# Where two pools begin in SBUF: activations 96 bytes, the MLP's stationary tiles 32 bytes past a multiple of 512

## The chip, the cores and the metric

The kernel runs on one core of one Trainium2 chip. The metric is the device time of one execution in microseconds (us); the median of two runs before the change is 1291.11 us (1289.03 and 1293.18).

## The reference

One decoder layer on x of 256 tokens by 2048, all in float32:

```
h   = x @ w_in                       # 2048 -> 7424
y_a = rwkv7_mix(h[:, :3328])         # 16 heads of 64: decay, in-context rate, state update, norm, gate
y_b = retention_mix(h[:, 3328:])     # 4 heads of 256: rotary, decayed scores, norm, swish gate
mix = concat(y_a, y_b) @ w_o         # 2048 -> 2048
x   = layer_norm(ALPHA * x + mix)
ff  = square(relu(x @ w_up)) @ w_down  # 2048 -> 8192 -> 2048
out = layer_norm(ALPHA * x + ff)
```

## The kernel before, in words

All weight matrices are streamed once from HBM as 202 chunks of 128 x 2048 floats (1 MB). A chunk comes as two halves: SP's queue loads a half into one of three `raw` tiles, ScalarE casts it to float32r as `whi` (L133), and VectorE writes the rest `raw - whi` as `wlo` (L135). `prefetch` (L119 ff.) keeps about one chunk ahead. Activations are held in the same two parts (`xh`/`xl` for x, `mxh`/`mxl` for the mixer's output, `x1h`/`x1l` after the first norm, `u0` and `uh`/`ul` for the squared ReLU), so a product of two matrices takes three TensorE matmuls for each 128 x 128 block: high by high, high by low, low by high. Every one of them comes with its own load of a stationary operand of 128 columns, 512 bytes in each partition.

Two forms carry nearly all of TensorE's time, and they differ in which side is stationary:

- `stat_tile` (L151): the weight block is stationary, and 256 columns of an activation move past it (1024 bytes per partition). 48 matmuls a chunk. Used for most of the input projection (40 tiles, `xh`/`xl`, 1920 matmuls; two more tiles at L377) and for the MLP's up projection (60 tiles, `x1h`/`x1l`, 2880 matmuls).
- `mov_chunk` (L167): 128 columns of an activation are stationary, and 512 columns of the weights move (2048 bytes). 24 matmuls a chunk. Used for retention's v and g (`xh`/`xl`, 384), for the output projection (`mxh`/`mxl`, 288), and for the MLP's down projection (`u0`, 96; `uh`/`ul`, 1344). `resident_block` (L187) is the same form for three blocks whose weights stay in SBUF as `wx` or `wb`.

In order of time: the input projection with the two mixers woven in (to about 453 us; their vector work runs on the other engines), the output projection (to about 556), the first norm and the first 512 columns of the up projection (to 586), then the MLP in four slices: L151 on `x1h`/`x1l`, then L167 on `uh`/`ul`, four times (586 to 1259); the last 512 output columns at L187 and the second norm end it.

Where a tile begins is set by the pools: each is laid out behind the pool before it, and each tile begins at a multiple of 32 bytes. Before the change the pool `big` holds four buffers of 16 KB under one tag; they are taken in turn by `xh`, `xl`, `mxh`, `mxl`, then `x1h`, `x1l`, `u0` and, at the end, the four `wb`. The pools behind it (`rp` of the mixers; `mp`, `wx`, `mp2` of what follows) begin where `big` ends; `mp` holds `stats2`, of which 60 of 108 floats are used.

Of the kernel before, what the change touches and what calls it, by code (L numbers as in the profile page):

```python
# [10 lines left out]
F32 = mybir.dt.float32  # L11
F32R = mybir.dt.float32r
# [5 lines left out]
P = 128  # L18
T = 256
D = 2048  # L20
KT = D // P
# [52 lines left out]
WO_ORDER = ((0, (0, 2)), (1, (0, 2)), (0, (1, 3)), (1, (1, 3)), (2, (0, 1, 2, 3)))  # L74
NS = 4

WO_LAST = 58 + 12

LAG = dict(lora=2, scan=3, sq=5, rn=1, kk=7, bt=2, g1=1, btok=1, ktok=2, g2=1, sub=3, xt=2, vtok=8, bg=4, d1=3, d2=1, f1=1, sa=2, st=2, yc=2)
# [21 lines left out]
def tile_hybrid_layer(ctx, tc, xT, xtok, ws, pp, lup, glup, ln1r, ln2r, cst, rope, dmask, eye, out):  # L101
# [2 lines left out]

    const = ctx.enter_context(tc.tile_pool(name="const", bufs=1))
    wp = ctx.enter_context(tc.tile_pool(name="wp", bufs=1))
    big = ctx.enter_context(tc.tile_pool(name="big", bufs=4))
    ps = ctx.enter_context(tc.tile_pool(name="ps", bufs=4, space=bass.MemoryType.PSUM))

    def mm_bank():  # L110
        return ps.tile([P, 512], F32, name="mm", tag="mm", bufs=4)

    def sm_bank():
        return ps.tile([P, 512], F32, name="sm", tag="sm", bufs=4)
# [6 lines left out]
    def prefetch(want=1):  # L121
        while len(ahead) < want and taken[0] < ws.shape[0]:
# [7 lines left out]
            for h, (hi, lo) in enumerate(parts):  # L130
                raw = wp.tile([P, 1024], F32, name="raw", tag="raw", bufs=3)
                nc.sync.dma_start(out=raw, in_=ws[i][:, 1024 * h:1024 * h + 1024])
                S.copy(hi, raw)  # L133
                E = G if (i - WO_LAST, h) in LO_G else V
                E.tensor_tensor(out=lo, in0=raw, in1=hi.bitcast(F32), op=ALU.subtract)  # L135
# [22 lines left out]
    def mov_chunk(act, dsts, first, last):  # L158

        ch = chunk()  # L160
        for tt in range(2):
            for k4 in range(4):
                hi, lo = ch[k4 // 2]
                c = slice(512 * (k4 % 2), 512 * (k4 % 2) + 512)
                ah, al = act(k4, tt)
                for j, (w, a) in enumerate(((hi, ah), (hi, al), (lo, ah))):
                    TE.matmul(dsts[tt], a, w[:, c], start=first and k4 == 0 and j == 0,  # L167
                              stop=last and k4 == 3 and j == 2)
                if tt == 1 and k4 == 1:
                    prefetch()  # L170
                if k4 % 2:
                    yield
# [22 lines left out]
    ppt = const.tile([P, NPP], F32, name="ppt")  # L195
    nc.scalar.dma_start(out=ppt, in_=pp)
    c1 = const.tile([P, NC1], F32, name="c1")
    xh = big.tile([P, KT * T], F32R, name="xh", tag="big")
    xl = big.tile([P, KT * T], F32R, name="xl", tag="big")
    def xact(kt):  # L200
        return xh[:, kt * T:kt * T + T], xl[:, kt * T:kt * T + T]

    def tok_act(ah, al, kq):
        def f(k4, tt):
            o = (4 * kq + k4) * T + P * tt
            return ah[:, o:o + P], al[:, o:o + P]
        return f

    mxh = big.tile([P, KT * T], F32R, name="mxh", tag="big")
    mxl = big.tile([P, KT * T], F32R, name="mxl", tag="big")  # L210

    ident = c1[:, C_ID:C_ID + 128]

# [622 lines left out]
    mp = ctx.enter_context(tc.tile_pool(name="mp", bufs=1))  # L836
# [4 lines left out]
    def run(gen):  # L841
        for _ in gen:
            pass

    def cb(n):
        return slice(512 * n, 512 * n + 512)
# [15 lines left out]

    stats = mp.tile([P, 2, 4, 6], F32, name="stats")

    stats2 = mp.tile([P, 108], F32, name="stats2")[:, 0:60].rearrange("q (a b c) -> q a b c", a=2, b=5)

    def residual(n, tt, bank):
        zs = z[:, tt, cb(n)]
        V.scalar_tensor_tensor(out=zs, in0=zs, scalar=ALPHA, in1=bank, op0=ALU.mult, op1=ALU.add)
        V.bn_stats(out=stats[:, tt, n], in_=zs)  # L870

    with ExitStack() as wctx:
        wx = wctx.enter_context(tc.tile_pool(name="wx", bufs=16))

        def kept():
            return [(wx.tile([P, 1024], F32R, name="wx", tag="wx"), wx.tile([P, 1024], F32R, name="wx", tag="wx"))
                    for _ in range(2)]

        for i in range(WO_LAST, WO_LAST + 8):
            place[i] = kept  # L880
        wo_banks = {}
        seen = {}
        for n, kqs in WO_ORDER:
            if n not in wo_banks:
                wo_banks[n] = [mm_bank(), mm_bank()]
                seen[n] = 0
            for kq in kqs:
                run(mov_chunk(tok_act(mxh, mxl, kq), wo_banks[n], seen[n] == 0, seen[n] == 3))
                seen[n] += 1
            if seen[n] == 4:  # L890
                for tt in range(2):
                    residual(n, tt, wo_banks[n][tt])

        x1h = big.tile([P, KT * T], F32R, name="x1h", tag="big")
        x1l = big.tile([P, KT * T], F32R, name="x1l", tag="big")

        def norm1(tt):
            mean, rs = center(tt, stats)
            for n in range(4):
                zs = z[:, tt, cb(n)]  # L900
                E = G if (tt, n) in NORM_G else V
                E.tensor_scalar(out=zs, in0=zs, scalar1=mean, scalar2=rs, op0=ALU.subtract, op1=ALU.mult)

        def turn1(tt, kqs):

            for kq in kqs:
                tb = sm_bank()
                for i in range(4):
                    kt = 4 * kq + i
                    ins = TE.transpose(tb[:, P * i:P * i + P], z[:, tt, P * kt:P * kt + P], ident)  # L910
                    if i == 0:
                        tc.keep_in_program_order(ins)
                tm = mp.tile([P, 512], F32, name="ltm", tag="ltm", bufs=2)
                for i in range(4):
                    kt = 4 * kq + i
                    o = slice(P * i, P * i + P)
                    if (tt, kq, i) in TURN_V:
                        V.tensor_scalar(out=tm[:, o], in0=tb[:, o], scalar1=pcol(L1W, kt), scalar2=pcol(L1B, kt),
                                        op0=ALU.mult, op1=ALU.add)
                    else:  # L920
                        S.activation(tm[:, o], tb[:, o], AF.Identity, bias=pcol(L1B, kt), scale=pcol(L1W, kt))
                dst = slice(4 * kq * T, 4 * (kq + 1) * T)
                xhv = x1h[:, dst].rearrange("q (k t) -> q k t", t=T)[:, :, P * tt:P * tt + P]
                xlv = x1l[:, dst].rearrange("q (k t) -> q k t", t=T)[:, :, P * tt:P * tt + P]
                tv = tm.rearrange("q (k t) -> q k t", t=P)
                S.copy(xhv, tv)
                E = G if (tt, kq) in TURN_G else V
                E.tensor_tensor(out=xlv, in0=tv, in1=xhv.bitcast(F32), op=ALU.subtract)

        chs = []
        for tt in range(2):
            bank = mm_bank()
            resident_block(lambda kq: tok_act(mxh, mxl, kq), [bank], chs, tt, (1, 2, 3, 4) if tt else (1, 1, 1, 0), tt == 1,
                           {MID0: lambda: turn1(0, range(4))} if tt else None)
            residual(3, tt, bank)
            norm1(tt)
        u0 = big.tile([P, KT * T], F32R, name="u0", tag="big")
        chs = []  # L940
        for tt in range(2):
            bank = mm_bank()
            resident_block(lambda kq: tok_act(x1h, x1l, kq), [bank], chs, tt, (1, 1, 1, 1), False,
                           None if tt else {MID1[0]: lambda: turn1(1, (0,)), MID1[1]: lambda: turn1(1, (1, 2, 3))})
            rl = mp.tile([P, 512], F32, name="ltm", tag="ltm", bufs=2)
            S.activation(rl, bank, AF.Relu)
            V.scalar_tensor_tensor(out=rl, in0=bank, scalar=0.0, in1=rl, op0=ALU.max, op1=ALU.mult)
            tb = sm_bank()
            for i in range(4):
                TE.transpose(tb[:, P * i:P * i + P], rl[:, P * i:P * i + P], ident)  # L950
            uh = u0[:, 0:1024].rearrange("q (k t) -> q k t", t=T)[:, :, P * tt:P * tt + P]
            ul = u0[:, 1024:2048].rearrange("q (k t) -> q k t", t=T)[:, :, P * tt:P * tt + P]
            tv = tb.rearrange("q (k t) -> q k t", t=P)
            S.copy(uh, tv)
            V.tensor_tensor(out=ul, in0=tv, in1=uh.bitcast(F32), op=ALU.subtract)
# [14 lines left out]
        return x1h[:, kt * T:kt * T + T], x1l[:, kt * T:kt * T + T]  # L970

    def kept2():
        t = [big.tile([P, KT * T], F32R, name="wb", tag="big") for _ in range(2)] if len(pair) == 0 else pair.pop()
        if len(t) == 2 and not isinstance(t[0], tuple):
            a, b = t
            pair.append([(a[:, 2048 + 1024 * i:3072 + 1024 * i], b[:, 2048 + 1024 * i:3072 + 1024 * i])
                         for i in range(2)])
            return [(a[:, 1024 * i:1024 * i + 1024], b[:, 1024 * i:1024 * i + 1024]) for i in range(2)]
        return t

    pair = []
    for i in range(ws.shape[0] - 4, ws.shape[0]):
        place[i] = kept2

# [79 lines left out]
def layout(inp):  # L1064
# [33 lines left out]
    for n, kqs in WO_ORDER:  # L1098
        for kq in kqs:
            mov(w_o[:, 512 * n:512 * n + 512], kq)  # L1100
    assert at[0] == WO_LAST
    for kq in range(4):
# [45 lines left out]
```

## Time and profile before

| | us |
|---|---|
| median of the two timed runs | 1291.11 |
| the profiled execution | 1294.34 |
| its span in the trace | 1292.5 |
| TensorE busy / VectorE / ScalarE / GpSimd | 1251.4 / 850.4 / 559.7 / 119.0 |
| up projection in the MLP, one slice of 768 matmuls at L151 | 92.15 |
| down projection in the MLP, one slice of 384 matmuls at L167 | 87.07 |

The profile is one execution, 3.2 us over the median. Starts of instructions are exact; a matmul's end is modelled, so the time that one costs is read from the distance between starts, not from its length. PE is TensorE's matmul, PEld its weight load, which runs beside the matmul ahead of it.

### The profile page before, as it was taken

How to read it: one execution, taken by the hardware profiler on the slowest of the kernel's cores; microseconds unless marked ns; L12 is line 12 of the kernel's file. 1: busy time of each engine (PE TensorE's matmuls, PEld its weight loads, DVE VectorE, ACT ScalarE, POOL GpSimd, SP SyncE). 2: the span in 40 equal slices, each digit the busy share in tenths (PEclk: the TensorE clock that was granted, in tenths of full speed). 3: DMA queues.
4: the chain of work that ended last, by engine and by line, in shares of the span. 5: the costliest groups of instructions: out<-in, count | busy, mean ns of one | idle time of the engine just before them, and what ended most of it. 6: DMA issues, size and time to landing. Idle time of an engine off the chain costs nothing.

```text
span 1292.5 us, 21924 instructions
## 1 busy us (share of the span) xinstructions
PE 1251.4 (97%) x8952; PEld 1128.9 (87%) x8952; DVE 850.4 (66%) x1311; ACT 559.7 (43%) x723; POOL 119.0 (9%) x97
## 2 busy tenths in 40 slices
PE   7998999999999999999999999999999999999996
PEld 7988889878999778779988899988999888999885
DVE  6898799799969756685654555545555554555566
ACT  5545335345434343464443344433444433444441
POOL 1100121110201100057300000000000000000001
PEclk9999999999999999999999999999999999999998
DMA  8565245355544436655655555555555555555562
GB/s 285 188 190 166 80 149 160 99 150 168 167 137 140 159 114 237 216 178 185 244 195 196 195 182 185 185 191 188 195 184 185 182 192 193 190 185 186 182 210 99
DMA packets 86185, 229.89 MB, mean 178 GB/s; under 512 B 30530, under 2 KB 30658, under 8 KB 85316
## 3 DMA queue, kind: packets, MB, share of 16 engines
q1 hardware_dynamic: 83924, 219.51, 51.7%
q0 software_dynamic: 1440, 7.87, 1.7%
q8 instruction: 70, 1.15, 0.3%
q10 hardware_dynamic: 720, 1.11, 0.3%
q14 instruction: 31, 0.25, 0.1%
HBM read 224.72 MB, written 3.74 MB: 177 GB/s over the span
## 4 chain that ended last, share of the span: by engine, by line
PE 81%; DVE 10%; DMA 4%; ACT 3%; issue 2%; POOL 1%; SPq 0%; DVEq 0%; ACTq 0%; POOLq 0%
PE mm L151 38%; PE mm L167 33%; PE mm L187 4%; DVE wlo L135 3%; DMA raw<-in_ws_dram 2%; DVE prod L673 1%; PE mm L377 1%; DVE xb L676 1%; PE sm L619 1%; DMA xt<-dxt 1%; ACT whi L133 1%; POOL qk L419 1%; DMA first<-in_ws_dram 1%; ACT wx L133 0%; PE sm L762 0%
## 5 line engine op out<-in xcount | busy, mean ns | idle before, releaser
L135 DVE TENSOR_TENSOR wlo<-raw,whi 128x1024 fp32r<-128x1024 f32 x375 | 465.7, 1243 | 338.2 <-ACT whi L133 328.6
L133 ACT CAST whi<-raw 128x1024 fp32r<-128x1024 f32 x376 | 394.4, 1050 | 560.7 <-PE mm L151 241.2
L151 PE MATMUL mm<-x1h,wlo 128*128 128x256 f32 x960 | 271.8, 283 | 0.0
L151 PE MATMUL mm<-x1l,whi 128*128 128x256 f32 x960 | 271.7, 283 | 0.0
L151 PE MATMUL mm<-x1h,whi 128*128 128x256 f32 x960 | 271.7, 283 | 0.0
L151 PE MATMUL mm<-xh,whi 128*128 128x256 f32 x640 | 186.2, 291 | 0.0
L151 PEld LDWEIGHTS mm<-x1l,whi 128*128 128x128 f32 x960 | 184.3, 192 | 0.2
L151 PEld LDWEIGHTS mm<-x1h,whi 128*128 128x128 f32 x960 | 184.3, 192 | 0.1
L151 PE MATMUL mm<-xl,whi 128*128 128x256 f32 x640 | 184.4, 288 | 0.0
L151 PEld LDWEIGHTS mm<-x1h,wlo 128*128 128x128 f32 x960 | 184.3, 192 | 0.0
L151 PE MATMUL mm<-xh,wlo 128*128 128x256 f32 x640 | 184.0, 287 | 0.0
L167 PE MATMUL mm<-whi,uh 128*128 128x512 f32 x448 | 174.3, 389 | 0.0
L167 PE MATMUL mm<-whi,ul 128*128 128x512 f32 x448 | 174.3, 389 | 0.0
L167 PE MATMUL mm<-wlo,uh 128*128 128x512 f32 x448 | 174.3, 389 | 0.0
L151 PEld LDWEIGHTS mm<-xh,whi 128*128 128x128 f32 x640 | 124.2, 194 | 2.9 <-issue 0.9
L151 PEld LDWEIGHTS mm<-xl,whi 128*128 128x128 f32 x640 | 124.5, 194 | 0.9 <-issue 0.2
L151 PEld LDWEIGHTS mm<-xh,wlo 128*128 128x128 f32 x640 | 124.3, 194 | 0.7
L167 PEld LDWEIGHTS mm<-wlo,uh 128*128 128x128 f32 x448 | 84.1, 188 | 17.5
L167 PEld LDWEIGHTS mm<-whi,uh 128*128 128x128 f32 x448 | 84.1, 188 | 17.4
L167 PEld LDWEIGHTS mm<-whi,ul 128*128 128x128 f32 x448 | 84.1, 188 | 17.3
L1038 POOL TENSOR_TENSOR z<-z,lnr 128x512 f32<-128x512 f32 x3 | 3.9, 1293 | 609.3 <-DVE stats L1026 609.3
L167 PE MATMUL mm<-whi,xh 128*128 128x512 f32 x128 | 51.6, 403 | 0.0
(270 smaller groups left out, 1613.1 us busy)
## 6 DMA issues: line engine op xcount, KB each, us to landing
raw<-in_ws_dram SPq DMA_DIRECT2D x400, 512.0 KB, 4.3
first<-in_ws_dram SPq DMA_DIRECT2D x8, 256.0 KB, 8.2
z<-in_xtok_dram POOLq DMA_DIRECT2D x2, 1024.0 KB, 10.6
lnr<-in_ln1r_dram POOLq DMA_DIRECT2D x2, 1024.0 KB, 5.5
lnr<-in_ln2r_dram POOLq DMA_DIRECT2D x2, 1024.0 KB, 10.7
xraw<-in_xT_dram SPq DMA_DIRECT2D x3, 512.0 KB, 8.8
dn<-g SPq DMA_DIRECT2D x8, 128.0 KB, 3.0
xt<-dxt SPq DMA_DIRECT2D x8, 128.0 KB, 4.1
```

The costliest lines, as they stand in the source:

```text
L133: S.copy(hi, raw)
L135: E.tensor_tensor(out=lo, in0=raw, in1=hi.bitcast(F32), op=ALU.subtract)
L151: TE.matmul(dst, w[:, c], a, start=n == 0, stop=n == 3 * KT - 1)
L167: TE.matmul(dsts[tt], a, w[:, c], start=first and k4 == 0 and j == 0, stop=last and k4 == 3 and j == 2)
L187: TE.matmul(dst, a, wt[:, o:o + w], start=kq == 0 and k4 == 0 and i == 0, stop=kq == 3 and k4 == 3 and i == 2)
L377: TE.matmul(lb[i][:, 0:T], w[:, c], a, start=kt == 0 and j == 0, stop=kt == KT - 1 and j == 2)
L419: G.tensor_tensor(out=o[:, hs[1]], in0=rb_[:, hs[0]], in1=rb_[:, hs[1]], op=ALU.add)
L619: TE.matmul(bank[r, 128 * n:128 * n + 128], src[r, c64(p, n)], ar[r, o:o + 128], start=True, stop=True)
L673: V.tensor_tensor(out=pv, in0=xbv[0:q, 0:m, 0:t], in1=blk.rearrange("q (s t) -> q t s", t=32)[0:q, t:t + 1, 0:t].broadcast_to([q, m, t]), ...
L676: V.tensor_reduce(out=xbv[0:q, 0:m, t], in_=pv, axis=AX.X, op=ALU.add)
L1038: G.tensor_tensor(out=z[:, tt, cb(n)], in0=z[:, tt, cb(n)], in1=lnr2[:, 0, cb(n)], op=ALU.mult)
```

## The change

No instruction is added, removed or moved: on all five engines the 12,250 instructions of the two programs stand in the same order, each with the same waits and the same semaphore updates. Only addresses differ.

```
+XGAP = 24
...
-    big = ctx.enter_context(tc.tile_pool(name="big", bufs=4))
+    big = ctx.enter_context(tc.tile_pool(name="big", bufs=1))
...
-    xh = big.tile([P, KT * T], F32R, name="xh", tag="big")
-    xl = big.tile([P, KT * T], F32R, name="xl", tag="big")
+    mxh = big.tile([P, KT * T], F32R, name="mxh", tag="mix", bufs=2)
+    mxl = big.tile([P, KT * T], F32R, name="mxl", tag="mix", bufs=2)
+    big.tile([P, XGAP], F32, name="gap", tag="gap", bufs=1)
+    xh = big.tile([P, KT * T], F32R, name="xh", tag="in", bufs=2)
+    xl = big.tile([P, KT * T], F32R, name="xl", tag="in", bufs=2)
...
-    stats2 = mp.tile([P, 108], F32, name="stats2")[:, 0:60].rearrange("q (a b c) -> q a b c", a=2, b=5)
+    stats2 = mp.tile([P, 92], F32, name="stats2")[:, 0:60].rearrange("q (a b c) -> q a b c", a=2, b=5)
...
-        x1h = big.tile([P, KT * T], F32R, name="x1h", tag="big")
+        x1h = big.tile([P, KT * T], F32R, name="x1h", tag="in", bufs=2)
...
-        u0 = big.tile([P, KT * T], F32R, name="u0", tag="big")
+        u0 = big.tile([P, KT * T], F32R, name="u0", tag="mix", bufs=2)
...
-        t = [big.tile([P, KT * T], F32R, name="wb", tag="big") for _ in range(2)] if len(pair) == 0 else pair.pop()
+        t = [big.tile([P, KT * T], F32R, name="wb", tag=homes[0], bufs=2) for _ in range(2)] if len(pair) == 0 \
+            else pair.pop()
...
-    pair = []
+    pair, homes = [], ["mix", "in"]
```

The 96 bytes of `gap` push `xh`, `xl` and all that lies behind them back by 96; `stats2`, shorter by 64, brings `wx`, `rl`, `uh` and `ul` to 32. The tile starts, as the programs have them, modulo 512:

| tiles | before | now |
|---|---|---|
| `whi`, `wlo`, `raw` (weights) | 0 | 0 |
| `mxh`, `mxl`, `u0`, first pair of `wb` | 0 | 0 |
| `xh`, `xl`, `x1h`, `x1l`, second pair of `wb` | 0 | 96 |
| `uh`, `ul`, `rl`, `lnr`, `wx` | 0 | 32 |
| `z` | 0 | 96 |
| mixers' scratch before `k` / from `k` on | 0 / 64 | 96 / 160 |

Three pairs of tiles in the kernel before are read by matmuls in plain float32: `qk0` and `qk1` begin at 64 both, `pm` at 64 and `vt` at 0, `z` at 0 and the identity at 128. `yc` begins at 96, `sq`, `kkr` and `a` at 0.

All slices of these tiles that a matmul reads begin at multiples of 512 bytes in the tile. So the moving operand began as far into its 512 bytes as the stationary one in every float32r matmul before, and now begins 96 further at L151 and L377, 96 (retention's v and g, x stationary), 32 (`uh`/`ul`) or 64 (first block of the up projection) less far at L167 and L187; 32 further where `wx` moves past `mxh`/`mxl`, and as before for the rest of the output projection and for `u0`. The four buffers are still taken over by the same tiles: `x1h` lies where `xl` lay, `x1l` where `xh`, `u0` where `mxl`, and `wb` first in the buffers of `mxh` and `u0`, then in those of `x1h` and `x1l`.

## Rows read from the trace of the kernel before

**Rows 1.** The page's parts 1 and 4: engines' busy time, the chain by line.

```profile
PE 1251.4 (97%) x8952; PEld 1128.9 (87%) x8952; DVE 850.4 (66%) x1311; ACT 559.7 (43%) x723; POOL 119.0 (9%) x97
...
PE 81%; DVE 10%; DMA 4%; ACT 3%; issue 2%; POOL 1%; SPq 0%; DVEq 0%; ACTq 0%; POOLq 0%
```

**Rows 2.** Chain in order of time, 586 to 1259 us: start, length, engine, line, count.

```profile
by line: PE mm L151 51.3%; PE mm L167 48.5%; PE mm L187 0.1%; PE sm L950 0.1%
...
655.91 87.07 PE mm L167 x384
742.98 92.15 PE mm L151 x768
```

**Rows 3.** Timeline of PE in a stretch at half clock: start, length, engine, line, tiles.

```profile
181.14 0.41 PE L151 MATMUL mm<-xh,whi 128*128 128x256 f32 x1
181.36 0.41 PE L151 MATMUL mm<-xl,whi 128*128 128x256 f32 x1
181.57 0.41 PE L151 MATMUL mm<-xh,wlo 128*128 128x256 f32 x1
...
182.42 0.41 PE L151 MATMUL mm<-xh,whi 128*128 128x256 f32 x1
```

**Rows 4.** Windows: us, PE, PEld, DVE, ACT, POOL busy, PEclk, DMA share, GB/s.

```profile
181.00:182.50 1.50, 1.50 (x9) 1.50 (x9) 0.76 (x3) 1.09 (x2) 0.61 (x1) 0.50 0.01 5
960.00:961.00 1.00, 1.00 (x10) 1.00 (x10) 0.38 (x1) 1.00 (x2) 0.00 (x0) 1.00 0.85 250
```

**Rows 5.** Timeline of PE: plain float32 matmuls (L430 to L443), transposes (L910).

```profile
183.50 0.59 PE L441 MATMUL sm<-vt,pm 128*128 128x256 f32 x2
183.93 0.59 PE L442 MATMUL sm<-vt,pm 128*128 128x256 f32 x2
184.36 0.59 PE L443 MATMUL sm<-vt,pm 128*128 128x256 f32 x2
...
266.15 0.38 PE L430 MATMUL sm<-qk,qk 128*128 128x256 f32 x1
266.36 0.61 PE L432 MATMUL sm<-qk,qk 128*128 128x128 f32 x4
...
551.45 1.91 PE L910 MATMUL sm<-c,z 128*128 128x128 f32 x16
```

**Rows 6.** Timeline of PE where L167 follows L151 in the MLP.

```profile
655.75 0.63 PE L167 MATMUL mm<-whi,u 128*128 128x512 f32 x2
656.22 0.39 PE L167 MATMUL mm<-wlo,u 128*128 128x512 f32 x1
656.44 0.63 PE L167 MATMUL mm<-whi,u 128*128 128x512 f32 x2
656.91 0.39 PE L167 MATMUL mm<-wlo,u 128*128 128x512 f32 x1
```

**Rows 7.** Groups of PE, ACT and DVE by shape: count, busy us, mean ns.

```profile
L910 PE MATMUL sm<-c,z 128*128 128x128 f32 x32 | 4.0, 274 | 0.0
...
L800 ACT ACTIVATE ysq<-yc 128x512 f32<-128x512 f32 x4 | 2.5, 630 | 11.9 <-DVE yc L799 11.9
...
L568 ACT ACTIVATE sq<-kkr 128x512 f32<-128x512 f32 x4 | 2.5, 628 | 0.6 <-DVE kkr L567 0.6
...
L806 DVE TENSOR_TENSOR yc<-yc,rsq_y 128x512 f32<-128x512 f32 x4 | 2.8, 688 | 0.0
L603 DVE TENSOR_TENSOR a<-a,kkr 128x512 f32<-128x512 f32 x4 | 2.7, 687 | 0.0
```

**Rows 8.** Chain by line, 24 to 453 us.

```profile
by line: PE mm L151 32.7%; PE mm L167 12.7%; DVE wlo L135 6.8%; DVE prod L673 4.0%; issue 4.0%; DVE xb L676 2.7%; PE sm L619 2.7%; DMA xt<-dxt 2.4%; POOL qk L419 1.7%; ACT whi L133 1.3%; PE sm L526 1.1%; DVE ra L413 1.1%; DMA raw<-in_ws_dra
```

**Rows 9.** Waits, 586 to 1259 us: who waited for whom, us in total, times, longest.

```profile
ACT whi L133 <- PE mm L167: 181.6, 114, 3.3
ACT whi L133 <- PE mm L151: 164.9, 101, 1.9
...
ACT whi L133 <- DMA raw<-in_ws_dram: 11.1, 5, 5.1
```

**Rows 10.** The page's parts 5 and 6: the weights' two passes, their loads.

```profile
L135 DVE TENSOR_TENSOR wlo<-raw,whi 128x1024 fp32r<-128x1024 f32 x375 | 465.7, 1243 | 338.2 <-ACT whi L133 328.6
L133 ACT CAST whi<-raw 128x1024 fp32r<-128x1024 f32 x376 | 394.4, 1050 | 560.7 <-PE mm L151 241.2
...
raw<-in_ws_dram SPq DMA_DIRECT2D x400, 512.0 KB, 4.3
```

More of the change, by code (lines that the diff above doesn't have):

```diff
@@ L207, in tok_act @@
         return f
-    mxh = big.tile([P, KT * T], F32R, name="mxh", tag="big")
-    mxl = big.tile([P, KT * T], F32R, name="mxl", tag="big")
     ident = c1[:, C_ID:C_ID + 128]
@@ L892, in tile_hybrid_layer @@
                     residual(n, tt, wo_banks[n][tt])
-        x1h = big.tile([P, KT * T], F32R, name="x1h", tag="big")
-        x1l = big.tile([P, KT * T], F32R, name="x1l", tag="big")
+        x1h = big.tile([P, KT * T], F32R, name="x1h", tag="in", bufs=2)
+        x1l = big.tile([P, KT * T], F32R, name="x1l", tag="in", bufs=2)
         def norm1(tt):
@@ L972, in kept2 @@
     def kept2():
-        t = [big.tile([P, KT * T], F32R, name="wb", tag="big") for _ in range(2)] if len(pair) == 0 else pair.pop()
+        t = [big.tile([P, KT * T], F32R, name="wb", tag=homes[0], bufs=2) for _ in range(2)] if len(pair) == 0 \
+            else pair.pop()
         if len(t) == 2 and not isinstance(t[0], tuple):
             a, b = t
+            homes.pop(0)
             pair.append([(a[:, 2048 + 1024 * i:3072 + 1024 * i], b[:, 2048 + 1024 * i:3072 + 1024 * i])
```

## The prediction

> **What bounds the kernel now.** The page comes first: TensorE is busy for 97% of the span and carries 81% of the chain that ended last [rows 1]. That alone doesn't say that its pace sets the time, since a matmul's end is modelled. The chain in order of time does: from 586 to 1259 us it is nothing but L151 and L167, in unbroken stretches of 768 matmuls in 92.15 us and 384 in 87.07 us [rows 2]. So in the MLP every nanosecond per matmul counts in full. The reader divides: 92.15 / 768 = 120.0 ns for 256 columns, 87.07 / 384 = 226.7 ns for 512. At the full clock (PEclk 1.00 in [rows 4], the 2.4 GHz level) the columns alone take 256 / 2.4 = 106.7 and 512 / 2.4 = 213.3 ns. Both forms thus pay the same **13.3 ns more per matmul**, whatever its columns: it goes with the weight load that each one has, not with what moves. It is the only thing here that an address could change: the 7,300 or so such matmuls carry some 98 us of it.
>
> When is it paid? In a stretch at half clock (PEclk 0.50 [rows 4], the 1.2 GHz level) the same L151 starts every (182.42 - 181.14) / 6 = 213.3 ns [rows 3], which is 256 / 1.2: nothing on top. Plain float32 matmuls, at full clock but half the columns per time, show hardly any either: four of 256 columns from 183.50 to 184.36 are 215 ns each, and 16 transposes in 1.91 us, the last of 0.27, are 109.3 ns each for 106.7 [rows 5, 7]. So the 13.3 ns appear only when float32r columns move at the full 4 bytes per cycle while the next weights are loaded: the two reads get in each other's way. That is my reading, not shown by a row.
>
> **What the change does, part by part.** No instruction is added, removed or moved, and the waits are the same, so nothing is queued behind anything new, no transfer starts earlier or later, and DMA, buffers and the order on each queue cost nothing by themselves. Three things have another address.
>
> (1) ScalarE and VectorE operands lie 96 or 32 bytes further on. The trace has such a pair: the square of `yc` (begins at 96) takes 630 ns against 628 for that of `kkr` (at 0), and the product into `yc` 688 against 687 [rows 7]. I take 0 us.
>
> (2) The weights' tiles `raw`, `whi`, `wlo` stay where they were, so their two passes (1,050 and 1,243 ns a half [rows 10]) stay too.
>
> (3) The relative position of TensorE's two reads. This has no row: in every float32r matmul of the trace both operands begin equally far into 512 bytes. What an offset is worth is therefore bounded from both sides. The low end is that the two reads no longer meet and 13.3 falls to the 2.7 ns of the transposes [rows 5, 7]: 10.7 ns less. The high end is the worst pace that L167 itself shows: in the first five after L151 the starts are (656.91 - 655.75) / 5 = 232 ns apart, 5.3 more than in the steady stretch [rows 6]. Between them I take **no change per matmul**, for three reasons from rows. The loss is the same for 256 and 512 columns, so it is counted per weight load, as a fixed number of reads that the moving side gives up; moving the start changes where in the stream they fall, not how many there are. A load runs beside a moving operand that covers 512 bytes again and again (two times in 1024, four times in 2048), so whatever the start, the two pass every relative position. And in plain float32 the pair that begins equally (L430 to L432, 0.21 us for 256 columns) and the pair 64 bytes apart (215 ns) go alike [rows 5]. Against it speak [rows 6]: there the pace depends on how the two streams happen to meet, for a few matmuls, before it locks in.
>
> The Trainium skill has a rule that speaks against the change more strongly (TensorE: Matmul & The Clock Gate, Step-by-step: what each phase is for): the array has two independent read ports, and loading the next weights takes no bandwidth from the running matmul. By it the sum below is 0 whatever the offset. The trace agrees only in part: [rows 3] show no loss, [rows 2] show 13.3 ns. The same page's section Back-to-back issue gap gives N / 2.4 + 2.5 ns, so 109.2 at 256 columns, an estimate of what would be left if nothing collided; the trace has that for transposes, not for float32r.
>
> **Sum:** 0 + 0 + 0. The profiled execution took 1294.3 us and lies 3.2 over the median of 1291.1; against the median the forecast is **1291 us**.
>
> **The rivals.**
>
> *Both offsets part the two reads.* 10.7 ns less for each of 2,880 matmuls at L151 on `x1h`/`x1l`: 30.8 us; for 1,344 at L167 and 48 at L187 on `uh`/`ul`: 14.9; for 96 more of half width at L187 and 96 with `wx`: 2.1; the MLP and its neighbours give 47.8. In the first 453 us only what is on the chain counts: L151 has 32.7% of 429 us, 140 us or 1,169 matmuls, L167 12.7%, 54.5 us or 240 [rows 8]; 1,409 x 10.7 = 15.1. Together 63 us: **1228 us**. The weights would keep up: a half of a chunk would last 24 x 109.3 = 2.62 us, ScalarE and VectorE need 1.05 and 1.24 for it, and a `raw` tile's round of 4.3 + 1.05 + 1.24 = 6.6 us fits into three halves, 7.9 [rows 10]; today ScalarE waits 346 us for TensorE and 11 for loads [rows 9]. For it: the loss vanishes at half pace, so it is a collision and not a fixed step, and equal starts may be its worst case. Against it: the three reasons above.
>
> *Only one offset does.* The moving 96 alone: 30.8 + 1,169 x 10.7 = 12.5, so 43 us and **1248**. The stationary 32 alone: 14.9 + 1.0 = 16 us, so **1275**, which is within 2%.
>
> *Slower.* Equal starts are the settled state that both forms fall into; a shift holds the streams in the meeting of [rows 6], 5.3 ns worse each. It decides as soon as that state no longer dies out after five matmuls. 4,464 matmuls of the MLP x 5.3 = 23.7 us, 1,409 before it 7.5: **1322**. For it: [rows 6] show such a state for this very form. Against it: it lasts 1.2 us each time. That it holds in part, at one of the two forms, would stay within 2%.
>
> *The change doesn't do what it says.* It does for the big groups; it leaves the output projection's `mxh`/`mxl` and `u0` at equal starts and moves `x` the other way round where x is stationary. These are 768 of the 7,300 and change the rivals' times by under 5 us.
>
> **How the numbers follow.** No effect 0.42; both offsets 0.20; only the moving one 0.14; only the stationary one 0.09; slower 0.15, of which 0.02 within 2%. A difference of 2%, 26 us, is about what a measurement here tells surely from none. Faster: 0.20 + 0.14 = 0.34. Within: 0.42 + 0.09 + 0.02 = 0.53. Slower: 0.13. Cases of both kinds hold much of the chance, so the range reaches to the fast one: 1226 to 1302; what it leaves out is mostly the slower rival. The likeliest case's own range is 1284 to 1298, the two timed runs and the profile with a few us on either side for a line more or less that a shifted tile takes.
>
> **What would show it.** Dividing the chain's stretches again: still 92 us for 768 and 87 for 384, and the forecast holds; 84 and 83, and the first rival does; about 96 and 89, and the slower one. If only the L151 stretches shrink, the offset of the moving side alone matters. ScalarE's `ysq` at 630 ns and the casts at 1,050 should not move. The forecast is wrong if the spacing of starts in the steady stretches changes by more than 3 ns.

## The result, and the profile after

The change takes **1307.71 us** (median; 1307.37 to 1308.05) where the kernel before takes 1291.11 (1289.03 to 1293.18): ratio 1.0108, 95% interval 1.0075 to 1.0141. So it is slower by 1.1%, 16.6 us: under the 2% line, but outside the range, whose upper end was 1302.

The profiled execution of the changed kernel took 1308.05 us, with a span of 1306.3. First the page's parts 1 and 4, which answer to [rows 1]. Two more lines ahead of them number L151 as L153, L167 as L169, L133 as L135 and L135 as L137; further down L187 is L189 and L800 is L805.

```profile
PE 1262.3 (97%) x8952; PEld 1127.9 (86%) x8952; DVE 854.1 (65%) x1311; ACT 560.0 (43%) x723; POOL 116.5 (9%) x97
...
PE 79%; DVE 10%; DMA 5%; ACT 3%; issue 2%; POOL 1%; SPq 0%; DVEq 0%; ACTq 0%; POOLq 0%
```

The counts are the same, TensorE is busy for 10.9 us more, and no other engine's busy time has moved by more than 4 us. The chain in order of time shows where (start, length, engine, line, count); it answers to [rows 2].

```profile
593.11 67.44 PE mm L153 x562
660.55 89.01 PE mm L169 x384
749.56 92.15 PE mm L153 x768
841.71 89.59 PE mm L169 x384
...
1205.21 67.19 PE mm L169 x288
```

The 256-column stretch has not moved: 92.15 us for 768, 120.0 ns each, as before. The 512-column one has gone from 87.07 to 89.59 us for 384, from 226.7 to **233.3 ns**. In the first slice 96 of its 384 have `u0` as the stationary operand, which the change leaves at an equal start, and so only 288 are longer: 89.01. Over the four slices, 288 + 384 + 384 + 288 = 1,344 matmuls at 6.6 ns more are 8.9 us, over half of the loss.

The timeline of PE where L169 follows L153 answers to [rows 6]; behind it stand four starts from the middle of that stretch.

```profile
660.39 0.62 PE L169 MATMUL mm<-whi,u 128*128 128x512 f32 x2
660.85 0.40 PE L169 MATMUL mm<-wlo,u 128*128 128x512 f32 x1
661.08 0.62 PE L169 MATMUL mm<-whi,u 128*128 128x512 f32 x2
661.54 0.39 PE L169 MATMUL mm<-wlo,u 128*128 128x512 f32 x1
...
715.02 0.40 PE L169 MATMUL mm<-wlo,uh 128*128 128x512 f32 x1
715.25 0.40 PE L169 MATMUL mm<-whi,uh 128*128 128x512 f32 x1
715.48 0.40 PE L169 MATMUL mm<-whi,ul 128*128 128x512 f32 x1
715.72 0.40 PE L169 MATMUL mm<-wlo,uh 128*128 128x512 f32 x1
```

The first ones, on `u0` (a `u` in the rows), start (661.54 - 660.39) / 5 = 230 ns apart and settle to 226.7; those on `uh` and `ul` stay at (715.72 - 715.02) / 3 = 233. Before, 232 ns lasted for five matmuls; now a pace close to it is the steady one. Whether the two are the same state, no row says. Inside the 256-column stretch the spacing of single matmuls was a constant 120 before and now cycles through values between 116 and 125, with the mean still 120.0.

The other engines' rows answer to [rows 7, 10] (groups by shape: count, busy us, mean ns).

```profile
L805 ACT ACTIVATE ysq<-yc 128x512 f32<-128x512 f32 x4 | 2.5, 631 | 11.8 <-DVE yc L804 11.8
...
L137 DVE TENSOR_TENSOR wlo<-raw,whi 128x1024 fp32r<-128x1024 f32 x375 | 467.3, 1247 | 344.3 <-ACT whi L135 342.3
L135 ACT CAST whi<-raw 128x1024 fp32r<-128x1024 f32 x376 | 394.8, 1050 | 571.5 <-PE mm L153 251.1
```

ScalarE's and VectorE's passes are unchanged within 4 ns. The first stretch of L169 in the MLP begins 4.6 us later in this profiled execution than in the one before (660.55 against 655.91). How much of that is the change, two single executions can't say.

### The profile page after: what moved, and what is told of

It is laid out like the page before. It is cut to its first block, busy times and chain, and to the rows that moved or that the text cites. A ratio compares the mean times of both kernels' runs of the same rounds, so it can differ in the third digit from the quotient of the medians.

```text
span 1306.3 us, 21924 instructions
## 1 busy us (share of the span) xinstructions
PE 1262.3 (97%) x8952; PEld 1127.9 (86%) x8952; DVE 854.1 (65%) x1311; ACT 560.0 (43%) x723; POOL 116.5 (9%) x97
## 4 chain that ended last, share of the span: by engine, by line
PE 79%; DVE 10%; DMA 5%; ACT 3%; issue 2%; POOL 1%; SPq 0%; DVEq 0%; ACTq 0%; POOLq 0%
PE mm L153 38%; PE mm L169 32%; DMA raw<-in_ws_dram 4%; PE mm L189 3%; DVE wlo L137 3%; PE mm L382 1%; DVE prod L678 1%; DMA xt<-dxt 1%; ACT whi L135 1%; DVE xb L681 1%; PE sm L624 1%; DMA first<-in_ws_dram 1%; POOL qk L424 1%; ACT wx L135 0%; DVE wx L137 0%
## 5 line engine op out<-in xcount | busy, mean ns | idle before, releaser
L137 DVE TENSOR_TENSOR wlo<-raw,whi 128x1024 fp32r<-128x1024 f32 x375 | 467.3, 1247 | 344.3 <-ACT whi L135 342.3
L135 ACT CAST whi<-raw 128x1024 fp32r<-128x1024 f32 x376 | 394.8, 1050 | 571.5 <-PE mm L153 251.1
L153 PE MATMUL mm<-x1l,whi 128*128 128x256 f32 x960 | 271.6, 283 | 0.0
L153 PE MATMUL mm<-x1h,wlo 128*128 128x256 f32 x960 | 270.9, 282 | 0.0
L153 PE MATMUL mm<-x1h,whi 128*128 128x256 f32 x960 | 269.6, 281 | 0.0
L153 PE MATMUL mm<-xh,whi 128*128 128x256 f32 x640 | 185.2, 289 | 0.0
L153 PE MATMUL mm<-xl,whi 128*128 128x256 f32 x640 | 183.4, 287 | 0.0
L153 PE MATMUL mm<-xh,wlo 128*128 128x256 f32 x640 | 182.8, 286 | 0.0
L153 PEld LDWEIGHTS mm<-x1h,whi 128*128 128x128 f32 x960 | 182.0, 190 | 0.1
L153 PEld LDWEIGHTS mm<-x1h,wlo 128*128 128x128 f32 x960 | 180.7, 188 | 0.0
L153 PEld LDWEIGHTS mm<-x1l,whi 128*128 128x128 f32 x960 | 179.7, 187 | 0.2
L169 PE MATMUL mm<-wlo,uh 128*128 128x512 f32 x448 | 177.2, 396 | 0.0
L169 PE MATMUL mm<-whi,ul 128*128 128x512 f32 x448 | 177.2, 395 | 0.0
L169 PE MATMUL mm<-whi,uh 128*128 128x512 f32 x448 | 177.2, 395 | 0.0
L153 PEld LDWEIGHTS mm<-xh,whi 128*128 128x128 f32 x640 | 121.9, 191 | 3.0 <-issue 0.9
L153 PEld LDWEIGHTS mm<-xh,wlo 128*128 128x128 f32 x640 | 122.5, 191 | 0.7
L153 PEld LDWEIGHTS mm<-xl,whi 128*128 128x128 f32 x640 | 122.0, 191 | 0.9 <-issue 0.2
L169 PEld LDWEIGHTS mm<-wlo,uh 128*128 128x128 f32 x448 | 84.2, 188 | 20.3
L169 PEld LDWEIGHTS mm<-whi,ul 128*128 128x128 f32 x448 | 84.2, 188 | 20.3
L169 PEld LDWEIGHTS mm<-whi,uh 128*128 128x128 f32 x448 | 84.2, 188 | 20.2
L169 PE MATMUL mm<-whi,xh 128*128 128x512 f32 x128 | 52.5, 410 | 0.0
## 6 DMA issues: line engine op xcount, KB each, us to landing
z<-in_xtok_dram POOLq DMA_DIRECT2D x2, 1024.0 KB, 10.9
lnr<-in_ln2r_dram POOLq DMA_DIRECT2D x2, 1024.0 KB, 10.9
```

The lines of the kernel that those rows point to most:

```text
L153: TE.matmul(dst, w[:, c], a, start=n == 0, stop=n == 3 * KT - 1)
```

## The experiments

Each ratio is to runs of the kernel before made beside the experiment: their median was 1290.43 us for experiments 2 and 3, 1291.33 for 4 and 6, and 1293.32 for 8. The kernels of matmuls alone (1, 5 and 7) were run once each.

**Theory A:** what counts is the relative start of the two operands, the stationary one's place against the moving one's. **Rival B:** an operand's own place counts. **Rival C:** no steady dependence; another engine or the transfers make the loss.

**1. A map of relative starts**, matmuls alone, 36 for each pair of places, at 512 and then at 256 columns.

```
REP = 36
...
    for n in (512, 256):
        for s, m in PAIRS:
            bank = ps.tile([P, 512], F32, name=name_of(n, s, m), tag="mm", bufs=4)
            for i in range(REP):
                so = s // 4 + 128 * (i % 16)
                mo = m // 4 + n * (i % (2048 // n))
                TE.matmul(bank[:, 0:n], sta[:, so:so + 128], mov[:, mo:mo + n], start=i == 0, stop=i == REP - 1)
```

> A kernel of matmuls alone: 47 pairs of starts (stationary, moving), each read by 36 float32r matmuls in a row, first with 512 moving columns, then with 256; it computes nothing of the reference. Theory A (relative start: only how much further one operand begins than the other counts): all pairs with equal starts, such as 32/32 and 96/96, go like 0/0, 226.7 ns at 512 columns and 120.0 at 256; pairs with a difference go at 233.3 ns at 512 columns whichever side is shifted. Theory B (each operand's own start: one that begins off a multiple of 64 bytes costs): 0/64, 64/0 and 128/128 go at 226.7 ns, every pair with a 32 or a 96 in it, 32/32 too, at 233.3. Theory C (a fixed number of reads per weight load, whatever the start, as forecast): all pairs at 226.7 and 120.0; the kernel after has already shown 233.3, so C can stand only if something else in it caused that. No theory says where, if anywhere, a pace under 226.7 or 117.7 is found; the map is to show it.

Its timeline has one row for each pair. In a name, the letters behind s and m count 32-byte steps of the stationary and the moving operand (a is 0, b 32, c 64, d 96, i 256); the length is that of 36 matmuls.

```profile
23.74 8.57 PE L62 MATMUL full_sa_mb<-mov,sta 128*128 128x512 f32 x36
82.42 8.35 PE L62 MATMUL full_sa_mi<-mov,sta 128*128 128x512 f32 x36
...
149.30 8.56 PE L62 MATMUL full_sb_ma<-mov,sta 128*128 128x512 f32 x36
...
274.70 8.36 PE L62 MATMUL full_sb_mb<-mov,sta 128*128 128x512 f32 x36
...
408.07 8.32 PE L62 MATMUL full_sa_ma<-mov,sta 128*128 128x512 f32 x36
...
441.83 4.28 PE L62 MATMUL half_sa_mg<-mov,sta 128*128 128x256 f32 x36
...
488.42 4.25 PE L62 MATMUL half_sc_ma<-mov,sta 128*128 128x256 f32 x36
492.51 4.49 PE L62 MATMUL half_sd_ma<-mov,sta 128*128 128x256 f32 x36
...
569.50 4.26 PE L62 MATMUL half_sd_mb<-mov,sta 128*128 128x256 f32 x36
...
616.14 4.48 PE L62 MATMUL half_sa_ma<-mov,sta 128*128 128x256 f32 x36
```

Both at 32 (8.36) goes like both at 0 (8.32) or like 256 apart (8.35), while 32 on either side alone costs 0.2 us; and at 256 columns the moving one at 192, the stationary one at 64, or 96 against 32 (all the same distance modulo 256) are equally fast. So A holds with a period of **256 bytes**, though not as I had put it (not every difference costs the same), and B falls. So does C, since nothing but matmuls runs here. The steady spacing, the mean over the last 24 matmuls of a pair, by moving less stationary place:

| columns | 0 | 32 | 64 | 96 | 128 | 160 | 192 | 224 |
|---|---|---|---|---|---|---|---|---|
| 512 | 226.7 | 233.3 | 228.9 | 233.3 | 233.3 | 234.4 | 233.3 | 233.3 |
| 256 | 120.0 | 117.8 | 117.8 | 120.0 | 118.8 | 117.4 | **113.3** | 118.3 |

At 512 columns all pairs of one distance agree within 0.8 ns. At 256 columns nearly all do, but three distances show two values: 32 has 117.8 and 116.7, 160 has 117.4 and 120.0 (the row with the stationary one at 96), and 192 has 113.3 four times and 117.8 once. I took these for strays; experiment 7 gives two values for 32 and for 192 again.

The change's two choices can be read off: 96 at 256 columns gives 120.0, what it was, and 32 on the stationary side, 224 here, gives 233.3 at 512 for 226.7.

**2. The moving offset alone:** `uh`, `ul` and `wx` go back to 0.

```diff
-    stats2 = mp.tile([P, 92], F32, name="stats2")[:, 0:60].rearrange("q (a b c) -> q a b c", a=2, b=5)
+    stats2 = mp.tile([P, 84], F32, name="stats2")[:, 0:60].rearrange("q (a b c) -> q a b c", a=2, b=5)
```

> Only the activations are moved (xh, xl, x1h, x1l at 96), uh, ul and wx are back at 0. If the 9 us that the MLP lost come from the stationary start alone: the slices at L169 on uh/ul take 87.1 us again, those at L153 92.15; what stays is retention's v and g (384 matmuls, up to 6.6 ns each, some 60% of it on the chain: 1.5 us) and the first block of the up projection (96 matmuls: 0.6 us): about 1293 us against 1291, ratio 1.002. If instead the shift of everything behind the pool costs (scratch, z, loads into tiles that begin at 96), the 4.6 us that the kernel after had lost by the MLP's start show here in full: ratio 1.0035 or more.

1294.85 us, ratio 1.0036 (1.0022 to 1.0050). The chain in the MLP is that of before:

```profile
743.17 92.16 PE mm L153 x768
835.33 87.08 PE mm L169 x384
```

The 4.6 us that remain lie outside these stretches: with `x` as the stationary operand (relative 160) L169 takes 234 ns instead of 228. Between 240 such matmuls (the chain before, [rows 8]) and some 350 (19% of this run's chain) count in the first 453 us; they make 1.4 to 2.1 us of it, and 96 on `wx`, at 234 for 229, another 0.5. The rest I can't place: the ratio is the one that I had set for a cost of moving everything behind the pool, but the profiled execution begins its slices only 0.2 us later than the one before (656.12 for 655.91), and experiment 4 moves everything by 32 bytes without a loss.

**3. The stationary offset alone**, in the kernel before.

```diff
-    stats2 = mp.tile([P, 108], F32, name="stats2")[:, 0:60].rearrange("q (a b c) -> q a b c", a=2, b=5)
+    stats2 = mp.tile([P, 116], F32, name="stats2")[:, 0:60].rearrange("q (a b c) -> q a b c", a=2, b=5)
```

> Only the MLP's stationary tiles and wx are moved to 32; xh, xl, x1h, x1l stay at 0. If the relative start of the two operands sets the pace at 512 columns: the slices at L167 take 89.6 us instead of 87.1 (u0's 96 matmuls apart), 9 us in all, with 0.6 us more for the 96 matmuls with wx: about 1300.5 us, ratio 1.007; L151 keeps 92.15. If the cost comes from the activations' 96: ratio 1.000.

1303.43 us, ratio 1.0091 (1.0068 to 1.0114), with the changed kernel's stretches:

```profile
748.64 92.14 PE mm L151 x768
840.78 89.59 PE mm L167 x384
```

The two parts add up: 0.0091 + 0.0036 = 0.0127 of 1291 is 16.4 us, for 16.6 of both. The loss is mostly the stationary one's 32 bytes.

**4. Everything at 32:** an early tile is longer, all weights and activations move with it.

```diff
-    dp = const.tile([P, 96], F32, name="dp")
+    dp = const.tile([P, 104], F32, name="dp")
```

> The kernel before with one early tile 32 bytes longer, so that weights, activations and everything behind them begin 32 bytes behind a line of 512: every relative start stays 0. Theory A (relative start alone): no change, 1287 to 1295, 120.0 and 226.7 ns. Rival B (an operand's own place counts, the change's stationary ones lost because they began at 32): 233 ns at the 512-column matmuls of uh and ul as with these alone at 32, 1299 to 1308.

1289.54 us, ratio 0.9998 (0.9981 to 1.0015). The place of an operand alone costs nothing in the full kernel either:

```profile
743.54 92.15 PE mm L151 x768
835.69 87.07 PE mm L167 x384
```

**5. A finer map:** the weights at 0, the moving operand in steps of 8 bytes, and two other widths.

```
FINE = [8 * i for i in range(32)]
PLAN = [(256, FINE + [180, 188, 196, 204, 0]), (512, FINE + [252, 0]),
        (128, [32 * i for i in range(8)]), (384, [32 * i for i in range(8)])]
...
    for n, moves in PLAN:
        for m in moves:
```

> Matmuls alone, as in the first map (it computes nothing of the reference): 36 float32r matmuls per start, the weights always at 0, the moving operand 0 to 248 bytes behind in steps of 8, at 256 and at 512 columns, then steps of 32 at 128 and 384 columns. Theory A (only the relative start within 256 bytes counts): what the first map gave comes back: at 256 columns 120.0 ns at 0, 113.3 at 192, 116 to 119 at 32, 64, 128, 160 and 224; at 512 columns 226.7 at 0, 228.9 at 64, 233.3 elsewhere; between them no start under 113.3 and 226.7. Rival D (finer steps have their own best): a start that is not a multiple of 32 is under 113 ns at 256 columns or under 226 at 512. If the spacing comes from the weight load and the stream meeting in a cycle, it depends on the columns too, so 128 and 384 columns have best starts of their own; if 192 is simply a good start, it is the best there as well.

Timeline rows as above; the first letter of a name counts 32 bytes, the second 4 (de is 112, ga 192, hc 232, cg 88).

```profile
75.76 4.30 PE L57 MATMUL half_de<-mov,sta 128*128 128x256 f32 x36
...
118.72 4.26 PE L57 MATMUL half_ga<-mov,sta 128*128 128x256 f32 x36
...
140.08 4.59 PE L57 MATMUL half_hc<-mov,sta 128*128 128x256 f32 x36
...
170.43 4.48 PE L57 MATMUL half_aa<-mov,sta 128*128 128x256 f32 x36
...
266.59 8.75 PE L57 MATMUL full_cg<-mov,sta 128*128 128x512 f32 x36
...
451.72 8.33 PE L57 MATMUL full_aa<-mov,sta 128*128 128x512 f32 x36
...
467.88 4.18 PE L57 MATMUL quar_ca<-mov,sta 128*128 128x128 f32 x36
...
483.96 4.18 PE L57 MATMUL quar_ga<-mov,sta 128*128 128x128 f32 x36
```

Steady spacings: 113.3 at 112 and at 192, up to 123.3 at 232; 512 columns 226.7 at 0 up to 240.0 at 88; no start below 113.3 or 226.7, so rival D falls. At 128 columns the start makes no difference (111.7), and at 384 the best are 0 to 64, 160 and 224 (173.3), the worst 96 (176.7), with 174.5 at 192: the best start depends on the columns.

**6. The moving ones at 192.**

```diff
-XGAP = 24
+XGAP = 48
...
-    stats2 = mp.tile([P, 92], F32, name="stats2")[:, 0:60].rearrange("q (a b c) -> q a b c", a=2, b=5)
+    stats2 = mp.tile([P, 60], F32, name="stats2")[:, 0:60].rearrange("q (a b c) -> q a b c", a=2, b=5)
```

> As the change, but x and x1 begin 192 bytes behind the weights' line instead of 96, and the MLP's stationary ones at 0 again (one size in another tile). Theory A: the 256-column matmuls of x and x1 take 113.3 ns instead of 120.0; 2880 of them in the MLP give 19.2 us; in the part ahead of the MLP some 1,900 more give 0 (other engines are late there) to 12.8 us; the 512-column ones on uh and ul go back to 226.7; those with x as the stationary operand stand at a relative 64 and take 228.9, some 250 of them, +0.6 us. Sum about 1265 us, 1258 to 1273, ratio to before 0.975 to 0.986. Rival E (the map does not carry over, since here ACT, DVE and the transfers use the same memory): 120 ns as before, 1291 to 1295. Rival F (the spacing falls, but the weights' transfers and casts become late): the 113.3 shows within steady stretches, with new idle ahead of the 256-column matmuls, and half of the 19 us or less is left, 1278 to 1285.

1283.35 us, ratio 0.9938 (0.9913 to 0.9962): faster than before, but 18 us over my 1265. Rival E falls. The time lies in rival F's band, yet not by its mechanism, for the stretches have no idle in them:

```profile
586.30 63.71 PE mm L153 x562
650.01 87.06 PE mm L169 x384
737.06 90.45 PE mm L153 x768
827.52 87.04 PE mm L169 x384
```

The first 256-column stretch has 63.71 / 562 = 113.4 ns, the later three 90.45 / 768 = 117.8, with the same places and the same code. What differs is what stands ahead: small matmuls in the first, 512-column ones in the others. The map at 192 had come from 256-column ones. So the map's number was not the whole rule.

**7. The same start behind different matmuls:** 12 of 512 columns at 0, then none, one of 128 or one of 64 columns, then 36 of 256 columns.

```
REP = 36
PRE = 12
...
PLAN = [("none", 0, [8 * i for i in range(32)] + [0]),
        ("wide", 128, [16 * i for i in range(16)]),
        ("slim", 64, [16 * i for i in range(16)])]
...
    for kind, extra, moves in PLAN:
        for m in moves:
            block("pre" + kind, 512, 0, PRE)
            if extra:
                block("put" + kind, extra, 0, 1)
            bank = block(kind, 256, m, REP)
```

> Matmuls alone (it computes nothing of the reference). Ahead of each 36 float32r matmuls of 256 columns, at one relative start each, stand 12 of 512 columns at relative 0, as in the MLP; then the same with one matmul of 128, or of 64 columns between the two. It asks why the version at 192 took 113.3 ns per 256-column matmul in its first stretch of the MLP, which small matmuls precede, and 117.8 in the three which follow the 512-column ones. Theory G (a relative start has more than one steady spacing, and the matmul ahead picks one): at 192 without an extra matmul 117.8, as in those three stretches; with one extra, 113.3 for at least one of the two widths. Rival H (something of the kernel beside the matmuls, such as the other engines' reads and writes or the transfers, makes the 117.8): 113.3 at 192 in all three. By G there may also be another start that takes 113.3 behind 512-column ones; the first two maps would put it near 112 or 192. At relative 0 both theories expect 120.0 each time.

```profile
116.93 4.28 PE L57 MATMUL none_de<-mov,sta 128*128 128x256 f32 x36
...
187.37 4.40 PE L57 MATMUL none_ga<-mov,sta 128*128 128x256 f32 x36
...
300.94 4.34 PE L57 MATMUL wide_de<-mov,sta 128*128 128x256 f32 x36
...
336.34 4.46 PE L57 MATMUL wide_ga<-mov,sta 128*128 128x256 f32 x36
...
414.68 4.37 PE L57 MATMUL slim_de<-mov,sta 128*128 128x256 f32 x36
...
450.09 4.35 PE L57 MATMUL slim_ga<-mov,sta 128*128 128x256 f32 x36
```

At 192 (ga) the steady spacing is 117.8 with none, 117.8 behind 128 columns and **113.3** behind 64: one relative start has two steady paces, and a single matmul ahead can pick one. At 112 (de) it is 113.3 behind all three, and at 0 it is 120.0. Theory G stands, without another engine in the kernel; rival H falls.

**8. Both consequences in the full kernel, side by side:** the moving ones at 112 (`x` and `x1` in one tile each, so that the 16 bytes fit), or at 192 with a 64-column matmul ahead of three stages. Both also take the MLP's stationary ones back to 0; the main lines of each edit are shown.

```diff
-    xh = big.tile([P, KT * T], F32R, name="xh", tag="in", bufs=2)
-    xl = big.tile([P, KT * T], F32R, name="xl", tag="in", bufs=2)
+
+    def inner(name):
+        t = big.tile([P, 2 * KT * T + 8], F32R, name=name, tag="in", bufs=1)
+        return t[:, 4:4 + KT * T], t[:, 4 + KT * T:4 + 2 * KT * T]
+
+    xh, xl = inner("x")
...
```

> The change with x and x1 112 bytes behind the weights' line instead of 96 (x, x1 and the last block's weights of that place each in one tile instead of two, their data 16 bytes into it) and the MLP's stationary ones at 0 again. By the third map 112 gives 113.3 ns at 256 columns behind every entry that was tried. Theory G: all 2880 256-column matmuls of the MLP at 113.3, that is 19.2 us less than before in them (rows 64 us for 562, 87.0 for 768); the 512-column ones with x as the stationary operand, relative 144, take 233 (some 250 of them, +1.5 us); in the part ahead of the MLP 0 to 6 us less. Sum 1264 to 1274, ratio 0.979 to 0.988. Rival I (the maps' 113.3 holds only in short stretches of one bank, and in a stage of 768 with three kinds of matmul 117 to 118 comes back): 87 us becomes 90.5, 1280 to 1285.

1273.60 us, ratio **0.9849** (0.9812 to 0.9886), with every stretch at 113.4 ns:

```profile
585.45 63.71 PE mm L153 x562
649.16 87.07 PE mm L169 x384
736.23 87.08 PE mm L153 x768
```

```diff
...
+        if sl:
+            TE.matmul(sm_bank()[:, 0:64], u0[:, 0:128], u0[:, 0:64], start=True, stop=True)
         while len(us) < 8:
```

> The version at 192 with one matmul more, of 64 columns, its result unused, ahead of the 256-column matmuls of the second, third and fourth slice of the MLP. Theory G (the matmul ahead picks one of two steady spacings): these three stages go from 117.8 to 113.3 ns, 768 each, 90.45 to 87.1 us, 10.2 us in all for 0.2 us of added matmuls: 1273 where the version at 192 took 1283, ratio to before 0.983 to 0.989. Rival H (something beside the matmuls in these stages makes the 117.8): the stages stay at 90.45, 1283.

1274.20 us, ratio 0.9851 (0.9810 to 0.9893). One more matmul per stage takes 3.3 us off it:

```profile
593.99 63.71 PE mm L153 x562
...
744.78 87.14 PE mm L153 x768
```

Its profiled execution took 1281.41 us, 7 us over the median (another of the six took 1281.61). That lies ahead of the added matmuls: the first stretch begins at 593.99 us, for 586.30 in the version at 192, though up to there the two kernels are the same. The two executions also differ in a pace there. Behind the same 512-column matmul L153 starts 120 matmuls, in the version at 192 (first row) 113.4 ns apart and here (second row), where TensorE had been idle for 0.22 us ahead of that matmul, 117.8:

```profile
43.15 0.40 PE L564 MATMUL sm<-lo,ones 128*128 128x512 f32 x1
...
44.62 0.50 PE L564 MATMUL sm<-lo,ones 128*128 128x512 f32 x1 [0.22 <-DVE lo L560]
```

So at 192 the shape of the matmul ahead is not all that decides.

Both gain what their stretches say: 67.44 - 63.71 and three times 92.15 - 87.08 are 18.9 us at 112, for 0.0151 x 1291 = 19.5 measured (15 to 24 by its interval).

## Why the prediction was wrong

**What bounds the kernel** was right, and it is why 6.6 ns per matmul show at all: the MLP's stretches stayed unbroken and took their changed pace in full.

**Terms (1) and (2)** were right: 631 ns for 630, casts of 1,050 and 1,247 for 1,050 and 1,243.

**Step (3), no change per matmul, failed.** It was put at 0. The runs showed 6.6 ns more for each 512-column matmul whose stationary operand moved by 32 bytes (226.7 to 233.3), 8.9 us in the MLP's slices, and no change of the mean at 256 columns. Its three reasons, one by one:

- *The loss is the same at both widths, so it is counted per weight load.* A coincidence of the one relative start that the trace had. Against 106.7 and 213.3 ns for the columns, the loss is 6.7 to 16.7 ns at 256 columns and 13.3 to 26.7 at 512, by the start.
- *The two pass every relative position, whatever the start.* Refuted by the maps: the pace goes by the distance of the starts modulo 256 bytes, and where several paces are possible it stays in the one that it fell into. [Rows 6] had shown two paces for one form, and I set the slower one aside as an entry that dies out.
- *Plain float32 goes alike at 0 and 64 apart.* True, and no evidence: that form showed no loss to begin with.

**The rivals.** The slower one came nearest: a shift that holds the two reads in a slower steady pace, 5.3 ns where 6.6 were measured, at the 512-column form. It charged the 256-column form too, which at 96 keeps 120.0 only by the choice of 96. Its half, at one form, had 0.02 of the chance; it is what happened. By its own price that half was 1,344 x 5.3 = 7.1 us, 1298 and inside the range. Two things carried it out: 6.6 for 5.3 ns (1.8 us), and the operands that I dropped as under 5 us, `x` as the stationary one and `wx`, which come with the moving offset: 4.6 us in experiment 2 (2.8 to 6.5 by its interval), of which I can name 1.9 to 2.6. The stationary offset cost 11.7 us in experiment 3, 2.8 more than its stretches show; its 192 matmuls on `wx` at 233 instead of 228 ns are 1.0 of that. The rest stays open. The part ahead of `wx` doesn't help: the first matmul on `wx` starts 2.6 us later than before in the changed kernel, 3.4 later in experiment 3 and 1.6 earlier in experiments 2 and 4, and neither 3 nor 4 alters a relative start on the way there, so single executions differ by that much.

The gain that the first rival hoped for, 10.7 ns at both forms, doesn't exist at any start that was run: the best is 6.7 ns at 256 columns, none at 512. Its idea that equal starts are a bad case was right for 256 columns, and 112 or 192 would have gained time with it.

**The skill's rule.** The maps bear on it: the same matmuls, with no other engine at work, take 113.3 to 123.3 ns by the distance of their two operands. The Trainium skill (TensorE: Matmul & The Clock Gate, Step-by-step: what each phase is for) says that loading weights takes no bandwidth from the running matmul. For float32r at full clock the traces do not agree, as the pace goes by where the two operands lie to each other. The prediction's estimate of 109.2 ns, from that page's section Back-to-back issue gap, was reached at no start.

**Not shown** is what inside TensorE or the memory makes the pattern. That the next weights' load and the moving stream collide would fit the missing loss at half clock [rows 3], but no run took the one without the other. At 128 columns the pace is 111.7 ns at every start tried, though half the columns move: there something else sets it, perhaps the one weight load that each matmul has. If so, it also keeps a 256-column matmul from the 109.3 ns that the first rival counted on.

## What to carry to other kernels

Where matmuls run back to back and set the time, the distance of their two operands modulo 256 bytes moves a 256-column float32r matmul by up to 9% (113.3 to 123.3 ns) and has to be measured for each width: what helps one width costs at another. Measure it behind the matmuls that really stand ahead, and prefer a start with one pace behind every entry tried (112 here) to one with two (192). And a pace that a trace shows for five matmuls only may be close to one that a small edit makes steady: give it its share of the chance, for each form by itself.

## What the runs showed of the hardware

- Spacing of float32r matmuls by relative start, period 256 bytes: 113.3 to 123.3 ns (256 columns), 226.7 to 240.0 (512), 173.3 to 176.7 (384, steps of 32), 111.7 throughout (128, steps of 32).
- One relative start can have two steady paces: 192 at 256 columns has 113.3 and 117.8, and held either for all 768 matmuls of a stage. Ahead of the MLP one stretch had 113.4 in one execution and 117.8 in another, behind the same matmul.
- A single 64-column matmul of 0.2 us switches it: 90.45 to 87.14 us a stage.
